# A two-layer transformer with 16 experts on one core: another order of work where the first expert stage opens, two weight tiles more, another last pair

## The chip, the core and the metric

The kernel runs on one core of a Trainium2 chip. The metric is device time in microseconds (us): 1926.18, the median of three runs (1924.14 to 1932.64). Five engines matter: TensorE (PE), VectorE (DVE), ScalarE (ACT), GpSimd (POOL) and SyncE (SP), which issues most of the transfers. About 0.5% of the time, 9.6 us, is what a measurement of this kernel can tell from no change.

## The reference

Two layers work on 512 latent tokens (`x`) and 256 context tokens (`ctx`) of width 1024. The second layer has no context output.

```
for l in range(2):
    need_ctx = l < 1
    mod_l = silu(c) @ w_mod[l] + b_mod[l]          # six vectors of 1024, and so for the context
    h_l = modulate(rms_norm(x, norm1_g[l]), sh1, sc1)
    y_l, y_c = token_mixer(h_l, h_c, w_in[l], ..., w_out[l], need_ctx)
    x = x + g1 * y_l
    h_l = modulate(rms_norm(x, norm2_g[l]), sh2, sc2)
    x = x + g2 * expert_choice_ffn(h_l, w_router[l], w_gate[l], w_up[l], w_down[l])
    if need_ctx: the same for ctx, with its own g1, sh2, sc2, g2
return rms_norm(x, final_g)

def expert_choice_ffn(h, ...):                     # 16 experts, each picks its best tokens
    aff = softmax(h @ w_router);  gate, idx = top_k(aff.T, cap)    # cap 64 latent, 32 context
    a, u = xs @ w_gate, xs @ w_up                  # xs = h[idx], matrices of 1024 x 1024
    y = (silu(a) * u) @ w_down * gate              # scattered back by idx, sums of all experts
```

All is float32. One layer's expert matrices are 16 x 3 x 4 MB.

## The kernel before

The program goes through six stages: the opening (loads, modulation vectors, norms), layer 0's mixer, layer 0's experts, and the same for layer 1 without an opening. Experts are taken two at a time, eight pairs `p` a layer.

**Weights.** Class `Ring` (L1426) streams the expert matrices. One load is half the rows (`kh`) of one expert's matrix, 128 partitions x 16 KB, 2 MB; two loads (both experts of the pair) make a half matrix. The loads' order is gate of pair 0, then up `p`, gate `p+1`, down `p` (`ring_loads`, L1415). They rotate through tiles: in layer 0 three in pool `ra` and three in `rb`, six. I count them from 0: loads 0 to 3 are gate of pair 0, 4 to 7 up of pair 0, 8 to 11 gate of pair 1, 12 to 15 down of pair 0. Load 6 takes load 0's tile. SP issues them in this order, and each waits until TensorE has read its tile for the last time.

**Expert stage of layer 0** (`experts`, L1181, with `two`). TensorE's order is written out. For pair 0 the latent gate product is made ahead (`gate0`, L1134, `ps_g`); in the stage itself come the first half of up (`ps_u`), the transposes of the context's gathered rows (`xsc`), the context's gate product (`ps_gc`), the second half of up, and the context's up product (`ps_uc`). Then pairs 1 to 7 go through gate, down and up, each half matrix with latent (`lat_mm`, L1117) and context (`cx_mm`, L1127) columns. Results of pairs 0 to 5 are scattered with addition into memory (`scatter`, L1287), those of 6 and 7 are added from PSUM (`add`, L1330) to `xe`, which is loaded after pair 5.

**Before that stage** stands the end of layer 0's mixer: the output projection (`acc`), `out_add` (L884), and for each stream the router: `Norm2` (L893) with squares on ACT, transposes `ps_t`, logits `ps_lg`, `softmax`, then `top` (L964, repeated max, replace and index of eight on DVE), and `slots_l` / `slots_c` (L998, L1030), which make the row indices by small matmuls `ps_r`. The latent selection ends first, its first gather is `xsl` and its transposes and modulation give `xT0`. The context's selection is woven between the matmuls of `gate0` by a scheduler; its scratch, its tile `xc` and the weight staging of the mixer lie in memory that the expert stage's pool `ep` takes over.

**Opening** (L1506 to L1530). SP loads six tiles `xt` of x and ctx (L284), small rows (`c`, `c_ctx`, `norm1_g`, `norm2_g`, `conv_w`, `final_g`) into tile `rows`, and then the modulation weights `wm` (L220) into four rotating buffers. `norm2_g` comes by four transfers that put every fourth number into a row (L1515). One transpose turns `rows` into `cols`, silu of which is `cT`, the operand of all modulation products `ps_mod` (`mod_half`, L210). ACT's six squares of `xt` and DVE's reciprocal roots (`rsqrt`, L171, 14 small instructions) normalise the tiles.

**Last pair of layer 1** (L1388 to L1407, `last_pair` L1145). The loop's last steps are `down(6)`, `up(7)`, `add(6)`, the transposes of the product (`turned(7)`), and `down(7)`. Between the halves of `down(7)` TensorE multiplies six of the eight 128x512 pieces of `x` by the identity into PSUM (`residual`):

```
PE.matmul(xa[t, h], ident, R.x[:, t, 512 * h:512 * h + 512], start=True, stop=False)
```

On top of them come the last pair's sums `yH` and `yL` (the high and the low part of the result). Two pieces are summed on DVE. Then follow squares on ACT, a reciprocal root for token tiles 0 and 1 and another for 2 and 3, the last product with `final_g` (five pieces on DVE, three on ACT and POOL), and eight stores.

Of the kernel before, what the change touches and what calls it, by code (L numbers as in the profile page):

```python
# [60 lines left out]
NACC = 6  # L61
FINE = (9, 10, 11, 12)
# [26 lines left out]
def kernel(ctx_stack: ExitStack, tc: tile.TileContext, x, c, ctx, c_ctx, w_mod, b_mod, norm1_g,  # L89
# [802 lines left out]
    class Norm2:  # L892
# [8 lines left out]

        def half(self, nh):
            s, p, pp, x, R = self.s, self.p, self.pp, self.x, self.R
            for t in range(NT[s]):
                xs = x[:, t, 512 * nh:512 * nh + 512]
                junk = p.tile([128, 512], BF, name="junk", tag="s2", bufs=S2O)
                ACT.activation(junk, xs, AF.Square, accum_out=self.sq[:, nh, t:t + 1])
                ps = pp.tile([128, 4, 128], F32, name="ps_t", tag="t", bufs=2)
                for j in range(4):
                    PE.transpose(ps[:, j], xs[:, j::4], ident)  # L910
                h = p.tile([128, 4, 128], F32, name="hsc", tag="s2", bufs=S2O)
                if t % 2:
                    DVE.tensor_copy(h, ps)
                else:
                    ACT.activation(h, ps, AF.Copy)
                yield
                for j in range(4):

                    js = slice(32 * j, 32 * j + 32)
                    PE.matmul(self.lg[js, 128 * t:128 * t + 128], R.wrA[s][:, 4 * nh + j, :], h[:, j],  # L920
                              start=(nh == 0 and t == 0), stop=(nh == 1 and t == NT[s] - 1), tile_position=(0, 32 * j))
                yield
# [211 lines left out]
    def gate0(gp, pp, ring, xl):  # L1134

        G = [pp.tile([128, 512], F32, name="ps_g", tag="acc", bufs=4) for _ in range(2)]
        W = [ring.get2() for _ in range(2)]
        for k in range(KC):
            lat_mm(G, xl, k, k % 4, W[k // 4], 64)
        sil = gp.tile([128, D], F32, name="sil0")  # L1140
        for h in range(2):
            ACT.activation(sil[:, 512 * h:512 * h + 512], G[h], AF.Silu)
        return sil, W

    def last_pair(ep, eq, pp, R, OH, yH, yL, xa, fg):  # L1145
# [14 lines left out]
        for t0 in range(0, NL, 2):  # L1160
            ts = slice(t0, t0 + 2)
            for t in range(t0, t0 + 2):
                for h in range(2):
                    junk = eq.tile([128, 512], BF, name="junk", tag="sil", bufs=1)
                    ACT.activation(junk, src[t, h], AF.Square, accum_out=m[:, 0, h, t:t + 1])
            DVE.tensor_tensor(m[:, 1, 0, ts], m[:, 0, 0, ts], m[:, 0, 1, ts], OP.add)
            rsqrt(m[:, 2, 0, ts], m[:, 1, 0, ts], m[:, 1, 1, ts], 1.0 / D)
# [12 lines left out]
    def experts(l, ep, ring, pp, R, xe, streams, late):  # L1180
# [15 lines left out]
        xT, sil, silc, aT, aTc, Y, G, GC, first, xs = {}, {}, {}, {}, {}, {}, {}, {}, [], {}  # L1196
# [43 lines left out]
        def up(p):  # L1240
            U = [ptile("ps_u", "b") for _ in range(2)]
            UC = ptile("ps_uc", "bc") if two else None
            for _ in matrix(U, UC, xT["l", p], two and lhs_c(xT["c", p], p)):
                pass
# [42 lines left out]
        def scatter(p, Dn, DC):  # L1287

            y = ep.tile([128, D], F32, name="y", tag=("yH", "yL")[p % 2], bufs=1)
# [11 lines left out]
            if p == NACC - 1:  # L1301
                for s in streams:
                    POOL.dma_start(xe[s], xres_d[s].rearrange("(t p) d -> p t d", p=128))

        def down(p, fill=None):
# [540 lines left out]
```

## Time and profile before

| | us |
|---|---|
| median of three runs | 1926.18 |
| the profiled execution, its own time | 1925.89 |
| its span, first to last instruction | 1924.1 |
| PE busy | 1783.6 (93%) |
| DVE busy | 664.1 (35%) |
| ACT busy | 481.9 (25%) |
| POOL busy | 321.1 (17%) |

| stage | from | to |
|---|---|---|
| opening, up to the first products of the mixer | 0 | 40 |
| layer 0's mixer and selection | 40 | 537 |
| layer 0's experts | 537 | 1060 |
| layer 1's mixer and selection | 1060 | 1440 |
| layer 1's experts and the last pair | 1440 | 1924 |

Layer 0's experts, in the 40 us from 800 to 840: PE busy 39.77, DMA 397 GB/s. Layer 1's experts, from 1600 to 1640: PE busy 38.66, DMA 430 GB/s. A matmul's end is modelled, so a busy PE may still be one that waits a little between instructions. The time that an engine waits for nothing visible is called issue.

### The profile page before, as it was taken

Reading aid. Unit: us, or ns where it says so; the run is one execution under the profiler, and the core shown is the slowest. Engines: PE = TensorE matmul, PEld = TensorE weight load, DVE = VectorE, ACT = ScalarE, POOL = GpSimd, SP = SyncE. Lnnn points to the kernel's source line nnn. Section 1 sums busy time; section 2 is a strip of 40 time slices with the busy share of each in tenths; the row PEclk is TensorE's granted clock in tenths of the full one; section 3 lists DMA queues with packets and bytes.
Section 4 is the critical chain, followed back from the end, with each engine's and each line's share of the span. In section 5 each row is a group of like instructions: output and inputs, shape, how many; then the busy total and the mean of one; then the engine's idle time right before and its main releaser. Section 6 shows DMA issues by size and latency. Waiting matters only on the chain. (4 is left out here: it accounts for less than half of the span.)

```text
span 1924.1 us, 30120 instructions
## 1 busy us (share of the span) xinstructions
PE 1783.6 (93%) x12613; PEld 1023.5 (53%) x12613; DVE 664.1 (35%) x1681; ACT 481.9 (25%) x965; POOL 321.1 (17%) x335
## 2 busy tenths in 40 slices
PE   4899999999889999999999889999969999999986
PEld 2787887767423333333323588887744444544432
DVE  5645435673611101011003655446341122221214
ACT  3344434353401001000000445454331000000001
POOL 3233123333200111011000233223410000000000
PEclk9999999999889999999999899999979999999998
DMA  7554264257659999999997411110747999999993
GB/s 236 167 198 166 91 205 155 88 187 291 272 214 422 410 410 415 417 399 401 402 412 318 155 45 42 59 34 34 294 176 277 427 429 430 430 430 429 429 429 145
DMA packets 90351, 527.63 MB, mean 274 GB/s; under 512 B 11300, under 2 KB 33880, under 8 KB 66408
## 3 DMA queue, kind: packets, MB, share of 16 engines
q1 hardware_dynamic: 84808, 511.24, 66.4%
q0 software_dynamic: 5408, 14.47, 2.6%
q8 instruction: 99, 1.62, 0.3%
q14 instruction: 36, 0.29, 0.0%
HBM read 510.41 MB, written 15.27 MB: 273 GB/s over the span
## 5 line engine op out<-in xcount | busy, mean ns | idle before, releaser
L1124 PE MATMUL ps_u<-ring,xTl 128*32 128x512 f32 (+1 forms) x1536 | 243.3, 601 | 14.2 <-DMA ring<-in_w_up_dram 13.5
L1124 PE MATMUL ps_g<-ring,xTl 128*32 128x512 f32 (+1 forms) x1472 | 239.0, 594 | 4.0 <-DMA ring<-in_w_gate_dram 2.8
L1124 PE MATMUL ps_d<-ring,aT 128*32 128x512 f32 (+1 forms) x1536 | 237.3, 593 | 2.5 <-DMA ring<-in_w_down_dram 2.1
L1124 PEld LDWEIGHTS ps_u<-ring,xTl 128*32 128x32 f32 (+1 forms) x1536 | 71.9, 120 | 169.3 <-issue 146.6
L1257 ACT ACTIVATE aT<-ps_t 128x512 f32<-128x512 f32 x16 | 9.6, 598 | 607.1 <-PE ps_t L1253 607.1
L353 PE MATMUL acc<-wH,hHl 128*128 128x256 f32 x512 | 152.4, 298 | 3.2 <-ACT wH L274 1.8
L1124 PEld LDWEIGHTS ps_g<-ring,xTl 128*32 128x32 f32 (+1 forms) x1472 | 74.3, 121 | 149.5 <-issue 130.5
L354 PE MATMUL acc<-wH,hLl 128*128 128x256 f32 x512 | 145.1, 283 | 3.2 <-DVE hLl L343 3.2
L1124 PEld LDWEIGHTS ps_d<-ring,aT 128*32 128x32 f32 (+1 forms) x1536 | 70.8, 119 | 145.0 <-issue 136.9
L355 PE MATMUL acc<-wL,hHl 128*128 128x256 f32 x512 | 145.6, 284 | 1.4 <-DVE wL L275 1.3
L353 PEld LDWEIGHTS acc<-wH,hHl 128*128 128x128 f32 x512 | 98.1, 192 | 30.8 <-issue 23.7
L1236 DVE TENSOR_TENSOR sil<-ps_u,sil 128x512 f32<-128x512 f32 x32 | 22.1, 692 | 244.6 <-PE ps_u L1124 233.4
L275 POOL TENSOR_TENSOR wL<-wraw,wH 128x512 fp32r<-128x512 f32 x44 | 57.5, 1308 | 275.1 <-ACT wH L274 253.6
L355 PEld LDWEIGHTS acc<-wL,hHl 128*128 128x128 f32 x512 | 98.1, 192 | 4.4 <-DVE wL L275 2.7
L354 PEld LDWEIGHTS acc<-wH,hLl 128*128 128x128 f32 x512 | 98.1, 192 | 4.1 <-DVE hLl L343 4.1
L1255 DVE COPY aT<-ps_t 128x512 f32<-128x512 f32 x16 | 11.1, 691 | 252.3 <-PE ps_t L1253 252.3
L1175 POOL TENSOR_TENSOR x<-z,xTl 128x512 f32<-128x512 f32 x3 | 4.2, 1412 | 501.8 <-ACT z L1174 501.8
L677 DVE TENSOR_REDUCE mc<-ps_s 128x1 f32<-128x513 f32 (+2 forms) x80 | 55.2, 690 | 84.3 <-PE ps_s L674 53.0
L679 ACT ACTIVATE P<-ps_s,mc 128x513 f32<-128x513 f32 (+2 forms) x80 | 55.1, 689 | 95.4 <-DVE mc L677 95.3
L274 ACT ACTIVATE wH<-wraw 128x512 fp32r<-128x512 f32 x88 | 55.0, 629 | 91.7 <-PE acc L354 43.4
L1114 PE MATMUL ps_x<-OT,xn 128*128 128x128 f32 x512 | 67.1, 297 | 8.1 <-DVE OT L1106 8.1
L1131 PE MATMUL ps_uc<-ring,xTc 128*32 128x512 f32 x512 | 72.9, 592 | 0.0
(492 smaller groups left out, 3201.3 us busy)
## 6 DMA issues: line engine op xcount, KB each, us to landing
ring<-in_w_up_dram SPq DMA_DIRECT2D x64, 2048.0 KB
ring<-in_w_gate_dram SPq DMA_DIRECT2D x61, 2048.0 KB
ring<-in_w_down_dram SPq DMA_DIRECT2D x61, 2048.0 KB
wm<-in_w_mod_dram SPq DMA_DIRECT2D x96, 512.0 KB
wraw<-in_w_in_dram SPq DMA_DIRECT2D x44, 512.0 KB
wraw_o<-in_w_out_dram SPq DMA_DIRECT2D x24, 512.0 KB
ring<-in_w_gate_dram SPq DMA_DIRECT2D x12, 512.0 KB
ring<-in_w_down_dram SPq DMA_DIRECT2D x12, 512.0 KB
```

The lines of the kernel that those rows point to most:

```text
L274: ACT.activation(H, src, AF.Copy)
L275: sub_eng().tensor_sub(L, src, f32(H))
L353: PE.matmul(ps, aH, bH, start=start, stop=False)
L354: PE.matmul(ps, aL, bH, start=False, stop=False)
L355: PE.matmul(ps, aH, bL, start=False, stop=stop)
L677: DVE.tensor_reduce(mc[:, 0:1], sc, AX.X, OP.max, negate=True)
L679: ACT.activation(P[:, :nk + 1], sc, AF.Exp, bias=mc[:, 0:1], accum_out=mc[:, 1:2])
L1114: PE.matmul(ps[:, j], R.xn[:, t, c0:c0 + 128], OT[:, t], start=(t == 0), stop=(t == 3))
L1124: PE.matmul(G[h][c:c + n], lhs[:, k, c:c + n], W[e][:, j, 512 * h:512 * h + 512], start=(k == 0), stop=(k == KC - 1), tile_position=(0, c))
L1131: PE.matmul(gcx[32 * b:32 * b + 32], lhs_c(k, e), W[e][:, j, 512 * h:512 * h + 512], start=(k == 0), stop=(k == KC - 1), tile_position=(0, ...
L1236: DVE.tensor_mul(sil[p][:, hs], U[h], sil[p][:, hs])
L1255: DVE.tensor_copy(aT[p][:, 4 * h:4 * h + 4], ps)
```

## The change

Four things change.

- **Opening.** `norm2_g` comes by one transfer of four rows of 512 numbers into a tile of its own, `rows2`, and four more transposes pick every fourth number. POOL clears `rows` first.
- **Selection.** TensorE's order in the opening of layer 0's expert stage is written out (`open_pairs`): the context's router transposes and logits, its softmax, the transposes of `xsl`, then `gate0` in three parts: two of its eight steps, the transposes of the affinities, four steps, the context's slots, two steps.
- **Ring.** Loads 6 and 7 get tiles of their own, in `ep`, of two halves each (four transfers of 1 MB). Rotation through the six tiles goes on with load 8. Later the same memory holds `y` and `xe`.
- **Last pair.** `add(6)` moves between the halves of `up(7)`. The identity products are gone: all eight sums are added to `x` on DVE, the last square is DVE's, and one reciprocal root serves all four token tiles.

```diff
+G0 = (2, 4)
...
-                    for i in range(4):
-                        SP.dma_start(rows[32 + 4 * i:36 + 4 * i], norm2_g[i // 2, 512 * (i % 2):512 * (i % 2) + 512]
-                                     .rearrange("(p j) -> j p", j=4))
+                    rows2 = p.tile([4, 512], F32, name="rows2", tag="s2", bufs=S2)
+                    SP.dma_start(rows2, norm2_g.rearrange("l (k n) -> (l k) n", n=512))
...
                     PE.transpose(ps[:, :68], rows, ident[:68, :68])
+                    for j in range(4):
+                        PE.transpose(ps[:, 128 + 4 * j:132 + 4 * j], rows2[:, j::4], ident[:4, :4])
                     DVE.tensor_copy(cols, ps[:, :68])
+                    DVE.tensor_copy(cols[:, 32:48].rearrange("p (b j) -> p b j", j=4),
+                                    ps[:, 128:144].rearrange("p (j b) -> p b j", j=4))
...
+                        def open_pairs():
+                            hs, todo = {}, [(h, t) for h in range(2) for t in range(2)]
+                            for i, ht in enumerate(todo):
+                                hs[ht] = nc2.turn(*ht)
+                                if i:
+                                    nc2.logits(*todo[i - 1], hs[todo[i - 1]])
+                            nc2.logits(*ht, hs[ht])
                             nc2.softmax()
-                            yield from keep("c", nc2, xc)
-                            slots_c(rp, pp, R, (yield from top(p, pp, R, "c", 32)), ra[0])
-                        aft = select_c()
+                            R.xT0 = columns(l, "l", R.xs0, ra[0], 1,
+                                            lambda nm: pp.tile([128, 512], F32, name=nm, tag="t", bufs=2))
+                            drain(keep("c", nc2, xc))
+                            g0 = gate0(ra[0], pp, ring, R.xT0, R)
+                            for _ in range(G0[0]):
+                                next(g0)
+                            tp = top(p, pp, R, "c", 32)
+                            next(tp)
+                            for _ in range(G0[1]):
+                                next(g0)
+                            try:
+                                while True:
+                                    next(tp)
+                            except StopIteration as e:
+                                slots_c(rp, pp, R, e.value, ra[0])
+                            drain(g0)
...
+                if self.n in self.extra:
+                    parts = self.extra.pop(self.n)
+                    for i, t in enumerate(parts):
+                        SP.dma_start(t, src[:, 2 * i:2 * i + 2])
+                    self.q[self.n] = Halves(parts)
+                    self.n += 1
+                    continue
...
+                if two:
+                    for i in range(2):
+                        ring.extra[6 + i] = [ep.tile([128, 2, D], F32, name="ring", tag=f"o{i}{j}", bufs=1)
+                                             for j in range(2)]
...
-                ps = xa[t, h] if t < 3 else pp.tile([128, 512], F32, name="ps_s", tag="a", bufs=2)
-                PE.matmul(ps, o_, yH[:, hs], start=(t == 3), stop=False)
+                ps = bank("ps_s")
+                PE.matmul(ps, o_, yH[:, hs], start=True, stop=False)
                 PE.matmul(ps, o_, yL[:, hs], start=False, stop=True)
-                src[t, h] = ps
-                if t == 3:
-                    src[t, h] = R.x[:, t, hs]
-                    DVE.tensor_add(src[t, h], src[t, h], ps)
+                src[t, h] = R.x[:, t, hs]
+                DVE.tensor_add(src[t, h], src[t, h], ps)
...
-                up(p + 1)
-            add(6)
+                up(p + 1, (lambda: add(6)) if p == 6 and not two else None)
+            if two:
+                add(6)
...
-            down(7, residual)
-            last_pair(ep, E[0], pp, R, OH, *Y[7], xa, fg)
+            down(7)
+            last_pair(ep, E[0], bank, R, OH, *Y[7], fg)
```

Where layer 0's expert stage opens, TensorE had this order before (a row is one line's matmuls in turn; `xsl` are the gathered latent rows, `xc` the context, `ps_lg` logits, `aff_c` affinities):

```order
L1088 MATMUL ps_t<-ident,xsl 128x128 x8
L1124 MATMUL ps_g<-ring,xTl 64x512
L910 MATMUL ps_t<-ident,xc 128x128 x8
L1124 MATMUL ps_g<-ring,xTl 64x512 x2
L920 MATMUL ps_lg<-hsc,wrAc 32x128 x8
L910 MATMUL ps_t<-ident,xc 128x128 x8
L1124 MATMUL ps_g<-ring,xTl 64x512 x2
L920 MATMUL ps_lg<-hsc,wrAc 32x128 x8
L1124 MATMUL ps_g<-ring,xTl 64x512 x2
L933 MATMUL ps_r<-qsum,lgs 128x16 x2
L1124 MATMUL ps_g<-ring,xTl 64x512 x6
L981 MATMUL ps_r<-ident,aff_c 16x128 x2
```

and has this one now:

```order
L911 MATMUL ps_t<-ident,xc 128x128 x8
L1026 MATMUL ps_r<-ident,tok_l 64x8 x2
L1026 MATMUL ps_r<-ident,val 64x8 x2
L1030 MATMUL ps_r<-ident,tok_l 64x8
L923 MATMUL ps_lg<-hsc,wrAc 32x128 x4
L911 MATMUL ps_t<-ident,xc 128x128 x4
L923 MATMUL ps_lg<-hsc,wrAc 32x128 x4
L911 MATMUL ps_t<-ident,xc 128x128 x4
L923 MATMUL ps_lg<-hsc,wrAc 32x128 x8
L942 MATMUL ps_r<-qsum,lgs 128x16 x2
L1097 MATMUL ps_t<-ident,xsl 128x128 x8
L1133 MATMUL ps_g<-ring,xTl 64x512 x8
```

The context's router now stands whole ahead of the gate products, and its first transposes even ahead of the latent slots (`tok_l`); before, 13 of the 32 gate matmuls stood ahead of the affinities, now 8.

At the end of the program, TensorE's order before, from the last sum of `add(6)` on (`sil` is the product of gate and up):

```order
L1338 MATMUL ps_s<-yH,OH 128x512
L1339 MATMUL ps_s<-yL,OH 128x512
L1253 MATMUL ps_t<-ident,sil 128x128 x8
L1124 MATMUL ps_d<-ring,aT 64x512 x16
L1405 MATMUL ps_x<-x,ident 128x512 x6
L1124 MATMUL ps_d<-ring,aT 64x512 x16
L1154 MATMUL ps_x<-yH,OH 128x512
L1155 MATMUL ps_x<-yL,OH 128x512
```

and now:

```order
L1355 MATMUL ps_s<-yH,OH 128x512
L1356 MATMUL ps_s<-yL,OH 128x512
L1133 MATMUL ps_u<-ring,xTl 64x512 x16
L1263 MATMUL ps_t<-ident,sil 128x128 x8
L1133 MATMUL ps_d<-ring,aT 64x512 x32
L1165 MATMUL ps_s<-yH,OH 128x512
L1166 MATMUL ps_s<-yL,OH 128x512
```

The second half of `up(7)` now follows `add(6)`, and nothing stands between the halves of `down(7)`. Elsewhere each engine's order is as before, but for ACT and DVE in the opening: ACT's last three squares of `xt` now follow the silu that makes `cT`, and DVE's copies into `cols` stand inside the first reciprocal root.

## Rows read from the trace of the kernel before

**Rows 1.** Timeline of SP, 0 to 48: start, us, engine, line, operation
```profile
5.59 9.91 SPq L1515 DMA_DIRECT2D rows<-in_norm_g_dram  x4
...
17.75 13.43 SPq L220 DMA_DIRECT2D wm<-in_w_mod_dram  x10
```
**Rows 2.** Stretch, us; busy PE, PEld, DVE, ACT, POOL; PEclk, DMA share, GB/s
```profile
12.00:14.00 2.00, 0.00 (x0) 0.00 (x0) 0.00 (x0) 1.57 (x3) 0.00 (x0) 1.00 0.26 2
```
**Rows 3.** Timeline of PE, 500 to 600; in brackets idle time before, and its releaser
```profile
512.83 1.98 PE L1088 MATMUL ps_t<-ident,xsl 128*128 128x128 f32 x8 [5.19 <-DMA xsl<-xn_l,idx_l]
...
519.38 1.23 PE L910 MATMUL ps_t<-ident,xc 128*128 128x128 f32 x8
...
523.14 0.62 PE L933 MATMUL ps_r<-qsum,lgs 128*128 128x16 f32 x4
...
537.24 7.07 PE L1124 MATMUL ps_u<-ring,xTl 128*32 128x512 f32 x64 [0.69 <-ACT sil L1142]
...
562.02 9.51 PE L1124 MATMUL ps_u<-ring,xTl 128*32 128x512 f32 x59 [3.12 <-DMA ring<-in_w_up_dram]
...
580.06 1.92 PE L1124 MATMUL ps_g<-ring,xTl 128*32 128x512 f32 x16
```
**Rows 4.** Stretches of 2 us, columns as in rows 2
```profile
564.00:566.00 2.00, 2.00 (x12) 0.39 (x8) 0.00 (x0) 0.00 (x0) 0.00 (x0) 0.50 0.98 418
...
574.00:576.00 2.00, 2.00 (x24) 0.54 (x20) 0.00 (x0) 0.00 (x0) 0.00 (x0) 1.00 0.00 0
```
**Rows 5.** Timeline of SP, 480 to 640
```profile
549.28 0.81 SPq L1463 DMA_DIRECT2D ring<-in_w_up_dram  x2
```
**Rows 6.** Timeline of PE, 1835 to 1925
```profile
1869.16 7.08 PE L1124 MATMUL ps_u<-ring,xTl 128*64 128x512 f32 x30 [2.61 <-DMA ring<-in_w_up_dram]
...
1880.06 1.35 PE L1253 MATMUL ps_t<-ident,sil 128*128 128x128 f32 x8
...
1888.57 5.42 PE L1405 MATMUL ps_x<-x,ident 128*128 128x512 f32 x12
1893.92 7.09 PE L1124 MATMUL ps_d<-ring,aT 128*64 128x512 f32 x32
```
**Rows 7.** Timeline of DVE, 1835 to 1925
```profile
1876.93 4.87 DVE L1340 TENSOR_TENSOR x<-x,ps_s 128x512 f32<-128x512 f32 x8
...
1901.73 1.45 DVE L1319 TENSOR_TENSOR yL<-ps_d,yH 128x512 fp32r<-128x512 f32 x2
...
1907.06 0.16 DVE L1166 TENSOR_TENSOR fm<-fm 128x2 f32<-128x2 f32 x1 [0.17 <-ACT junk L1165]
...
1909.62 0.75 DVE L1177 SCALAR_TENSOR_TENSOR x<-ps_x,fm,xTl 128x512 f32<-128x512 f32 x1
...
1915.81 2.41 DVE L1177 SCALAR_TENSOR_TENSOR x<-x,fm,xTl 128x512 f32<-128x512 f32 x2
```
**Rows 8.** Timeline of ACT, 0 to 48
```profile
10.79 1.06 ACT L296 ACTIVATE junk<-xt 128x1024 bf16<-128x1024 f32 x1 [0.22 <-DMA xt<-in_ctx_dram]
...
12.41 1.06 ACT L296 ACTIVATE junk<-xt 128x1024 bf16<-128x1024 f32 x1 [0.47 <-DMA xt<-in_ctx_dram]
```
**Rows 9.** Timeline of DVE, 0 to 48
```profile
20.19 0.23 DVE L1521 COPY cols<-ps_t 128x68 f32<-128x68 f32 x1 [8.34 <-PE ps_t L1520]
...
26.48 1.42 DVE L302 TENSOR_SCALAR xt<-xt,rstd 128x1024 f32<-128x1024 f32 x2
```
**Rows 10.** Timeline of POOL, 496 to 590
```profile
506.10 1.26 POOL L890 TENSOR_TENSOR xc<-xc,ty 128x512 f32<-128x512 f32 x1 [1.67 <-DVE ty L889]
...
509.49 1.27 POOL L890 TENSOR_TENSOR xc<-xc,ty 128x512 f32<-128x512 f32 x1
```
**Rows 11.** Stretch of 1 us near the end, columns as in rows 2
```profile
1889.00:1890.00 1.00, 1.00 (x4) 0.41 (x3) 0.00 (x0) 0.00 (x0) 0.00 (x0) 1.00 0.17 66
```
**Rows 12.** Timeline of ACT, 1835 to 1925
```profile
1908.50 0.63 ACT L1165 ACTIVATE junk<-x 128x512 bf16<-128x512 f32 x1
```
**Rows 13.** Timeline of POOL, 1835 to 1925
```profile
1910.63 2.49 POOL L1175 TENSOR_TENSOR x<-z,xTl 128x512 f32<-128x512 f32 x2 [498.90 <-ACT z L1174]
```

More of the change, by code (lines that the diff above doesn't have):

```diff
@@ L900, in __init__, with turn, logits @@
             self.lg = pp.tile([128, 512], F32, name="ps_lg", tag="lg", bufs=1)
-        def half(self, nh):
[L903 to L915, printed above, removed]
+        def turn(self, nh, t):
+            p = self.p
+            xs = self.x[:, t, 512 * nh:512 * nh + 512]
+            junk = p.tile([128, 512], BF, name="junk", tag="s2", bufs=S2O)
+            ACT.activation(junk, xs, AF.Square, accum_out=self.sq[:, nh, t:t + 1])
+            ps = self.pp.tile([128, 4, 128], F32, name="ps_t", tag="t", bufs=2)
+            for j in range(4):
+                PE.transpose(ps[:, j], xs[:, j::4], ident)
+            h = p.tile([128, 4, 128], F32, name="hsc", tag="s2", bufs=S2O)
+            if t % 2:
+                DVE.tensor_copy(h, ps)
+            else:
+                ACT.activation(h, ps, AF.Copy)
+            return h
+        def logits(self, nh, t, h):
+            for j in range(4):
+                js = slice(32 * j, 32 * j + 32)
+                PE.matmul(self.lg[js, 128 * t:128 * t + 128], self.R.wrA[self.s][:, 4 * nh + j, :], h[:, j],
+                          start=(nh == 0 and t == 0), stop=(nh == 1 and t == NT[self.s] - 1), tile_position=(0, 32 * j))
+        def half(self, nh):
+            for t in range(NT[self.s]):
+                h = self.turn(nh, t)
                 yield
[L917 to L921, printed above, removed]
+                self.logits(nh, t, h)
                 yield
@@ L1238, in times, with up @@
                 DVE.tensor_mul(silc[p], UC, silc[p])
[L1240 removed]
+        def up(p, fill=None):
             U = [ptile("ps_u", "b") for _ in range(2)]
             UC = ptile("ps_uc", "bc") if two else None
[L1243 removed]
+            for _ in matrix(U, UC, xT["l", p], two and lhs_c(xT["c", p], p), fill=fill):
                 pass
@@ L1301, in scatter, with down @@
             if p == NACC - 1:
-                for s in streams:
-                    POOL.dma_start(xe[s], xres_d[s].rearrange("(t p) d -> p t d", p=128))
-        def down(p, fill=None):
+                y2 = ep.tile([128, 2, D], F32R, name="yHL", tag="o00", bufs=1)
+                last.extend(y2[:, i] for i in range(2))
+                xr = [ep.tile([128, 2, D], F32, name="xe", tag=f"o{g}", bufs=1) for g in ("01", "10", "11")]
+                xe["l"], xe["c"] = Halves(xr[:2]), xr[2]
+                for i, s in enumerate("llc"):
+                    POOL.dma_start(xr[i], xres_d[s][256 * (i == 1):256 * (i == 1) + 256, :].rearrange("(t p) d -> p t d", p=128))
+        def down(p):
             Dn = [ptile("ps_d", "a") for _ in range(2)]
             DC = ptile("ps_dc", "ac") if two else None
-            for _ in matrix(Dn, DC, aT[p], lambda k, e: aTc[p][:, k % 4, 2 * e + k // 4, :], fill=fill):
+            for _ in matrix(Dn, DC, aT[p], lambda k, e: aTc[p][:, k % 4, 2 * e + k // 4, :]):
                 pass
@@ L1369, in experts @@
                     cx_mm(UC, lc, k, k % 4, W1[k // 4])
+                y2 = ep.tile([128, 2, D], F32, name="y", tag="o00", bufs=1)
+                ys.extend(y2[:, i] for i in range(2))
                 silu(0)
@@ L1510 @@
                     rows = p.tile([68, 128], F32, name="rows", tag="s2", bufs=S2)
+                    POOL.memset(rows, 0.0)
                     SP.dma_start(rows[0:8], c.rearrange("b (r p) -> (b r) p", p=128))
```

63 lines of the change are left out of this document (34 added, 29 removed).

## The prediction

> **What bounds the kernel now.** I read the page's shares first: PE is busy for 93% of the span. So only stretches in which PE waits, or works at half speed, can give time, and there are three of them that the change touches.
>
> The first is the start. SP's timeline shows the four `norm2_g` transfers at 5.59, holding SP for 9.91 us, and the first `wm` issued at 17.75 [rows 1]. In the stretch from 12 to 14 the DMA moves 2 GB/s [rows 2]: nothing of weight is under way, and PE has nothing to multiply.
>
> The second is layer 0's expert opening. PE's timeline shows the order of things and the waits: `xsl` transposes at 512.83, first `ps_u` at 537.24, then the second half of up held by DMA (the last of its waits is 3.12) until 562.02, and pair 1's gate at 580.06 [rows 3]. The windows show the rest: at 564 to 566 PE works at a granted clock of 0.50, and at 574 to 576 no DMA runs although PE is full [rows 4]. So loads 6 and 7 came too late, not too slowly. SP issued them at 549.28 [rows 5]: they sit in the tiles of loads 0 and 1, which the context's gate product reads until then. After this stage opens, PE is full (39.77 of 40 us in the table above), so what PE gains here stays gained. Layer 1's experts run at the DMA's pace instead, but their loads follow the mixer's end and move with it as a block.
>
> The third is the end. PE's timeline has a wait of 2.61 for up's second half at 1869.16, then `add(6)` behind it, then 5.42 us of identity products between the halves of `down(7)` [rows 6]. DVE's timeline has the tail behind the last product at 1901.01 [rows 7].
>
> The profiled execution took 1925.89, 0.29 below the median of the runs; I make the sum against it.
>
> **Start: 5.5 less.** The four transfers go, and one of four long rows comes, which I cost like its neighbours: below 1 us of SP's time. In the built order SP then waits, before each further transfer, for an earlier one to complete; the first `wm` stands behind the first context tile. That tile had landed at 10.79, the other at 12.41 [rows 8]. So `wm` starts up to 17.75 − 10.79 = 7.0 earlier. That is the upper end. What may not keep up is the normalised x, which PE transposes among the products. Before, `rows` were copied at 20.19, and the last tile was scaled from 26.48 in two of 1.42, done by 27.9 [rows 9]: 7.7 us in all, beside `wm` transfers that hid it. After the change ACT makes three of the six squares behind `cT`, so at best they come at 12.41 + 1.5 (landing of the rows, the transposes) + 3 × 1.25 = 17.7, and DVE then needs 7.7 less one early pair's 1.3, until 24.1: 3.8 earlier than 27.9. This is the lower end while DVE is late. PE has products of its own to put between, so I take the middle, 5.5. The four extra transposes, the second copy and POOL's clearing lie in the wait for the first weights; bare, they would cost under 1 us.
>
> **Opening of the experts: 14.2 less.** Here PE's order is fixed, so I lay it out in the trace's time. The context's last sums are made on POOL; the first tile's end at 507.36, the last piece at 509.49 + 1.27 = 510.76 [rows 10]. The transposes of the first now stand ahead of the latent slots. Half of 1.23 behind 507.36 is 508.0, some 0.85 later for the slots by my estimate, and so for POOL's gather and last sum behind them: 511.6. From there to the softmax's products stand four transposes, a copy, eight logits matmuls. In the trace the stretch from 519.38 to 523.14 + 0.62 holds all that and eight gate products of 0.22 [rows 3] [rows 6]: 4.4 with them, 2.6 without. I take 4.0: the `xsl` transposes begin at 515.6, 2.8 later than before, and end at 517.5 (1.98 for eight, against 1.35 for eight at the end of the program, so at the low clock).
>
> Then gate 0: 64 products at 7.09 for 32, 14.2. I add 1.3 for a start at the low clock, 1.2 for two groups of small products between its parts (0.62 for such a group), 0.7 for silu as before: `ps_u` at 534.9, against 537.24. From there to pair 1's gate stand four products of 64 at 7.07 and two sets of transposes at 1.35: 31.0 without a wait, so 565.9 where the trace has 580.06. **That is 14.2.**
>
> Is the load there? Loads 6 and 7 lie in memory that the context's scratch holds until the context's slots are made. Those stand behind six of the eight gate steps on PE: 517.5 + 1.3 + 0.6 + 6 × 1.77 = 530.0, so I put the issue at 530.5. They need 10 us for 4 MB at the 418 GB/s of [rows 4], so they land by 541 to 543, with the two gathers among them. The second half of up wants them behind 534.9 + 7.07 + 1.35 + 7.07, at 550.4. Seven us are spare. Load 8 and the later ones then find their tiles free as before, and the DMA, idle at 574 to 576, has its work earlier. The context's gather, delayed by that traffic, is wanted only at 542. SP's queue holds the two loads ahead of gate 1's, which could not start before 549 anyway.
>
> Bounds: without lateness and low clock, 512.83 + 1.98 + 14.2 + 1.2 + 0.7 + 31.0 = 561.9, which is 18.2 less. At half clock through all of gate 0, 12.9 more than I reckon: 1.3 less.
>
> **End: 7.9 less.** `add(6)` took 3.8 (1876.24 to 1880.06) and moves into the wait of 2.61: the second half of up starts at 1866.55 + 3.8 instead of 1869.16 and ends at 1877.4. Its product takes 0.7, the transposes and copies 1.5: `down(7)` starts at 1879.6 instead of 1881.56. DVE's sums of pair 6 (4.87 for eight) now run beside PE. With the identity products' 5.4 gone, the last product ends at 1893.6 instead of 1901.0, 7.4 earlier. The last weights don't hold it: from 1889 to 1890 the last 66 GB/s come in [rows 11], and the last quarter of the second half is read only after 1891.
>
> The tail: before, from the last product to DVE's last one 17.2, and 5.9 of stores behind. After (E is the last product): both sums' parts by E + 2.2 as now, eight sums at 0.61 until E + 7.1, seven squares on ACT, 0.63 each [rows 12] and 0.75 with their read-out, until E + 8.1, a reciprocal root of 2.56 until E + 10.7, then five products on DVE. All of them now read `x` and `final_g` from SBUF. From PSUM one took 0.75; the two from SBUF took 2.41, 1.2 each, beside POOL's sum. POOL's two of 1910.63 took 2.49 [rows 13]. Five at 1.2 end at E + 16.7: 0.5 less than before. All at 0.75 would give 2.8 less; five of these and three of POOL's one after another, 3.8 + 3.7, end at E + 18.2: 1.0 more. I take 0.5 less, the rows' own price.
>
> That last case is a rule of the Trainium skill, "SBUF — State Buffer", section "SBUF: two separate sides": a VectorE operation with two SBUF inputs and a GpSimd operation hold their shared port pair in turn, each blocking the other for its whole length. By it the end would give 6.4 in place of 7.9, and the sum 1899.8. The 2.41 agrees with some blocking, not with a full turn each.
>
> The loads of `xe` in three transfers, and `y` in one tile, lie beside PE's full stretch and cost nothing as long as PE does not wait there.
>
> **Sum:** 5.5 + 14.2 + 7.9 = 27.6. 1925.9 − 27.6 = **1898.3**.
>
> **Rivals.**
> - *The start is absorbed.* DVE's normalising, late behind `cT`, is then what PE waits for, and the gain is nil: 1903.8. For it: DVE's 7.7 us; against it: PE has the products first.
> - *Gate 0 stays slow.* The selection in front leaves PE mostly idle, and gate 0 runs at the low clock: 1.3 in place of 14.2, so 1911.2. For it: `xsl` transposes at 1.98. Against it: PE is dense from 517.5 on.
> - *Only the end holds.* The loads come no earlier, since the memory stays held by something that I overlooked, or layer 1 takes back what layer 0 gives: 1918.0, within 0.5%.
> - *Slower: the low clock through the whole opening.* If the small steps keep PE at half speed for gate 0 and the four products behind it, 14.2 + 4 × 7.07 − 1.3 = 41.2 more turn 27.6 into −13.6: 1939.5. It decides from 27.6 us of lost speed on. Against it: at 564 to 566 the clock was 0.50 after a wait, and at 574 to 576 it was 1.00 again [rows 4].
>
> The Trainium skill, "TensorE: Matmul & The Clock Gate", Part 1, says that the slow clock is the default and that activity lifts it. By that rule a thinner stretch ahead of gate 0 costs time, which the last and the second rival price from rows; the 0.50 at 564 to 566, behind a wait, agrees.
>
> **How the numbers follow.** Forecast 0.65, start absorbed 0.14, gate 0 slow 0.12, only the end 0.06, slower 0.03. The forecast's own bounds: all upper ends give 7.0 + 18.2 + 10.2 = 35.4, so 1890.5. The range goes from there to 1911, which takes in the first rival and half of the second. About 0.5%, 9.6 us, is what a measurement can tell from no change: faster 0.91, same 0.06, slower 0.03.
>
> **What would show it.** `wm` from 11 on and the first `ps_mod` by 16; loads 6 and 7 issued near 525 (all that follows the start is 5.5 earlier), no DMA wait in the second half of up, pair 1's gate near 560; both halves of `down(7)` end to end; the tail about 22.6 from the last product to the end. It is wrong if PE's first transposes of x wait for DVE, if a granted clock of 0.50 lasts through gate 0, if the loads are issued only where the gate's tiles come free, or if DVE's last products and POOL's sums alternate in full.

## The result, and the profile after

The changed kernel took 1898.55 us in the median of four runs (1895.8 to 1900.76), the kernel before 1927.58 beside it. The ratio is 0.9847, with a 95% interval of 0.982 to 0.9874. Measured once more with the last experiments it took 1899.8 against 1924.56, a ratio of 0.9874 (0.9858 to 0.9889). The forecast was 1898.3.

| | before | after |
|---|---|---|
| the profiled execution, its own time | 1925.89 | 1895.8 |
| its span | 1924.1 | 1894.0 |
| PE busy | 1783.6 | 1772.5 |
| POOL busy | 321.1 | 323.1 |

**The start.** SP's timeline of the changed kernel from 0 to 48: the one `norm2_g` transfer takes 0.25 where four held SP for 9.91, and the first `wm` goes out at 10.34 instead of 17.75 [rows 1].

```profile
5.48 0.25 SPq L1546 DMA_DIRECT2D rows<-in_norm_g_dram  x1
7.72 0.30 SPq L1547 DMA_DIRECT2D rows<-in_conv_w_dram  x1
9.06 0.27 SPq L1548 DMA_DIRECT2D rows<-in_final_g_dram  x1
10.34 17.08 SPq L221 DMA_DIRECT2D wm<-in_w_mod_dram  x10
```

From 12 to 14 the DMA moves 260 GB/s instead of 2 [rows 2]. TensorE's timeline of the same stretch:

```profile
15.57 7.30 PE L225 MATMUL ps_mod<-wm,cT 128*32 128x512 f32 x20 [0.67 <-ACT cT L1557]
...
23.41 0.33 PE L309 MATMUL ps_t<-ident,xt 128*128 128x128 f32 x1 [0.17 <-DVE xt L303]
24.67 0.33 PE L309 MATMUL ps_t<-ident,xt 128*128 128x128 f32 x1 [0.93 <-DVE xt L303]
25.62 0.41 PE L309 MATMUL ps_t<-ident,xt 128*128 128x128 f32 x2 [0.62 <-DVE xt L303]
...
34.89 0.39 PE L354 MATMUL acc<-wH,hHl 128*128 128x256 f32 x1 [1.20 <-ACT wH L275]
```

Here are three waits on DVE's normalising, 1.7 together. The prediction named such waits as a sign that it is wrong; the gain came all the same. The last row is the first product of the mixer; it stood at 40.24 before. The 7.30 of the modulation products ahead of the waits are mostly waits as well: TensorE's weight loads (PEld) show 1.77, 1.11, 1.15 and 1.47 for `wm`, 5.5 together. The first of these rows and the last:

```profile
17.53 0.19 PEld L225 LDWEIGHTS ps_mod<-wm,cT 128*32 128x32 f32 x4 [1.77 <-DMA wm<-in_w_mod_dram]
...
21.82 0.14 PEld L225 LDWEIGHTS ps_mod<-wm,cT 128*32 128x32 f32 x4 [1.47 <-DMA wm<-in_w_mod_dram]
```

**The opening of the experts.** TensorE's timeline from 485 to 600, to be read beside [rows 3]:

```profile
509.75 1.95 PE L1097 MATMUL ps_t<-ident,xsl 128*128 128x128 f32 x8
511.63 4.32 PE L1133 MATMUL ps_g<-ring,xTl 128*64 128x512 f32 x16
...
516.20 7.09 PE L1133 MATMUL ps_g<-ring,xTl 128*64 128x512 f32 x32
...
528.16 7.07 PE L1133 MATMUL ps_u<-ring,xTl 128*32 128x512 f32 x64 [0.70 <-ACT sil L1152]
...
543.40 7.05 PE L1133 MATMUL ps_u<-ring,xTl 128*32 128x512 f32 x64
...
558.55 1.92 PE L1133 MATMUL ps_g<-ring,xTl 128*32 128x512 f32 x16
```

The second half of up starts without a wait, and pair 1's gate at 558.55 instead of 580.06. SP's timeline has loads 6 and 7, in four parts, 16 us ahead of the gate's loads; the windows show full speed and a busy DMA where [rows 4] had a clock of 0.50 and a DMA at rest:

```profile
523.93 2.17 SPq L1476 DMA_DIRECT2D ring<-in_w_up_dram  x4
540.19 4.24 SPq L1493 DMA_DIRECT2D ring<-in_w_gate_dram  x4
```

```profile
543.00:545.00 2.00, 2.00 (x24) 0.62 (x20) 0.00 (x0) 0.60 (x1) 0.00 (x0) 1.00 0.98 418
552.00:554.00 2.00, 2.00 (x24) 0.64 (x20) 0.00 (x0) 0.00 (x0) 0.00 (x0) 1.00 1.03 442
```

**The end.** TensorE's timeline (as [rows 6]), and below it its weight loads, which show what the first product of `down(7)` waits for:

```profile
1835.54 7.08 PE L1133 MATMUL ps_u<-ring,xTl 128*64 128x512 f32 x30 [2.42 <-DMA ring<-in_w_up_dram]
...
1846.52 7.09 PE L1133 MATMUL ps_u<-ring,xTl 128*64 128x512 f32 x32
1853.54 1.60 PE L1263 MATMUL ps_t<-ident,sil 128*128 128x128 f32 x8
1855.07 1.07 PE L1133 MATMUL ps_d<-ring,aT 128*64 128x512 f32 x2
1856.97 13.95 PE L1133 MATMUL ps_d<-ring,aT 128*64 128x512 f32 x62 [0.82 <-DMA ring<-in_w_down_dram]
```

```profile
1856.96 0.20 PEld L1133 LDWEIGHTS ps_d<-ring,aT 128*64 128x64 f32 x4 [1.70 <-DMA ring<-in_w_down_dram]
```

`add(6)` stands between 1842.6 and 1846.5 as planned, and both halves of `down(7)` run end to end. New is the wait of 1.70 for down's weights, which the prediction did not have. DVE's and POOL's timelines of the tail:

```profile
1872.98 4.86 DVE L1168 TENSOR_TENSOR x<-x,ps_s 128x512 f32<-128x512 f32 x8
...
1881.56 6.42 DVE L1187 SCALAR_TENSOR_TENSOR x<-x,fm,xTl 128x512 f32<-128x512 f32 x5
```

```profile
1882.36 5.07 POOL L1185 TENSOR_TENSOR x<-z,xTl 128x512 f32<-128x512 f32 x3 [494.69 <-DVE x L1187]
```

DVE's five products are of two kinds, as the list of their lengths in ns (least, median, most) shows: 0.75 us before POOL starts, 1.75 beside it. Each engine's queue closes the program with instructions called DRAIN (L1900). POOL's longest lasts 8267 ns. It begins at 1884.9 and ends at 1893.2, 5.7 behind POOL's last product; SP is at its first DRAIN, behind the stores, at 1891.0:

```profile
L1187 DVE SCALAR_TENSOR_TENSOR x<-x,fm,xTl x5: 744/1746/1750, 1881.6 to 1886.2; 128x512 f32<-128x512 f32 x5
L1900 POOLq DRAIN  x3: 51/97/8267, 1884.9 to 1893.7; - x3
L1900 SPq DRAIN  x3: 7/7/7, 1891.0 to 1893.4; - x3
```

**Where the time went.** The same program does not put its stages at the same time in each execution, so I compare distances inside one execution. The marks are: the first product of the mixer; the last product of the context's output projection (505.78 before, 500.01 after); the first `ps_u` of pair 0; pair 1's gate; the first half of `up(7)`; the end of the last `ps_d`; the span's end.

| stretch | before | after | gain | forecast |
|---|---|---|---|---|
| to the mixer's first product | 40.24 | 34.89 | 5.35 | 5.5 |
| to the output projection's last | 465.54 | 465.12 | 0.4 | 0 |
| to the first up | 31.46 | 28.15 | 3.3 | 2.3 |
| to pair 1's gate | 42.82 | 30.39 | 12.4 | 11.9 |
| to `up(7)` | 1279.4 | 1277.0 | 2.4 | 0 |
| to the last `ps_d`'s end | 41.55 | 35.38 | 6.2 | 7.4 |
| to the span's end | 23.1 | 23.1 | 0.0 | 0.5 |

(The forecast's 14.2 of the opening is split here by its own numbers: 537.24 − 534.9 = 2.3, and the rest, 14.2 − 2.3 = 11.9.) This is one pair of executions; three of its rows look different over all runs, as the experiments show: the start, the end, and the stretch to `up(7)`.

### The profile page after: what moved, and what is told of

Its sections match the earlier page's. It is cut to its first block, busy times and chain, and to the rows that moved or that the text cites. A ratio compares the mean times of both kernels' runs of the same rounds, so it can differ in the third digit from the quotient of the medians.

```text
span 1894.0 us, 30111 instructions
## 1 busy us (share of the span) xinstructions
PE 1772.5 (94%) x12605; PEld 1017.2 (54%) x12605; DVE 664.9 (35%) x1676; ACT 480.9 (25%) x963; POOL 323.1 (17%) x337
## 5 line engine op out<-in xcount | busy, mean ns | idle before, releaser
L1133 PE MATMUL ps_u<-ring,xTl 128*32 128x512 f32 (+1 forms) x1536 | 238.8, 592 | 4.1 <-DMA ring<-in_w_up_dram 3.4
```

The source lines that it names most:

```text
L1133: PE.matmul(G[h][c:c + n], lhs[:, k, c:c + n], W[e][:, j, 512 * h:512 * h + 512], start=(k == 0), stop=(k == KC - 1), tile_position=(0, c))
```

## The experiments

Eleven variants and the changed kernel once more. Times are medians; the kernel before is the one of the same call.

| run | us | before | ratio (95%) |
|---|---|---|---|
| 1 order alone | 1911.17 | 1925.29 | 0.9925 (0.9909 to 0.9942) |
| 2 tiles alone | 1901.51 | 1925.29 | 0.9874 (0.9858 to 0.9891) |
| 3 old start | 1901.56 | 1925.29 | 0.988 (0.9863 to 0.9896) |
| 4 old end | 1906.9 | 1925.29 | 0.9903 (0.9883 to 0.9923) |
| 5 normalising first | 1900.78 | 1924.4 | 0.9875 (0.9859 to 0.9892) |
| 6 `add(6)` back | 1900.7, one run | 1924.4 | |
| 7 tail on DVE | 1896.78, one run | 1924.4 | |
| 8 `down(7)` in quarters | 1899.86 | 1924.4 | 0.9869 (0.9853 to 0.9886) |
| 9 squares first | 1900.94, one run | 1924.56 | |
| 10 = 7 and 8 | 1896.28 | 1924.56 | 0.9851 (0.9836 to 0.9867) |
| 11 = 10, `up(7)` in quarters | 1896.74 | 1924.56 | 0.9846 (0.9827 to 0.9864) |
| 12 changed kernel again | 1899.8 | 1924.56 | 0.9874 (0.9858 to 0.9889) |

### 1 and 2: order of work or tiles?

Run 1 takes the two tiles away; run 2 weaves the context's selection into gate 0 as before, with the tiles.

```diff
-                    for i in range(2):
-                        ring.extra[6 + i] = [ep.tile([128, 2, D], F32, name="ring", tag=f"o{i}{j}", bufs=1)
-                                             for j in range(2)]
+                    pass
```

> The changed kernel without the two extra weight tiles: TensorE's new order stays, loads 6 and 7 go back to the tiles of loads 0 and 1. Theory (the tiles carry most of the opening's 15.7 us): the loads are issued only when the context's gate product has read the first tiles, near 540, the second half of up ends some 12 us later than in the changed kernel, pair 1's gate starts near 570 instead of 558.6, and the profiled time is near 1908. Rival (the order carries it): pair 1's gate within 4 us of 558.6, time below 1900.

```diff
-                        def open_pairs():
...
+                        def select_c():
+                            for h in range(2):
+                                yield from nc2.half(h)
+                            nc2.softmax()
+                            yield from keep("c", nc2, xc)
+                            slots_c(rp, pp, R, (yield from top(p, pp, R, "c", 32)), ra[0])
+                        aft = select_c()
```

> The changed kernel with the old weaving of the context's selection into gate 0, but with the two extra tiles. Theory: up starts 3.3 us later than in the changed kernel (near 531.5), loads 6 and 7 are issued near 527.5 and arrive in time, pair 1's gate starts near 562, and the profiled time is near 1899. Rival (without the order the tiles' memory comes free too late): a wait on DMA in the second half of up, pair 1's gate after 566, time above 1903.

TensorE's timeline of run 1, then of run 2:

```profile
530.86 7.07 PE L1133 MATMUL ps_u<-ring,xTl 128*32 128x512 f32 x64 [0.70 <-ACT sil L1152]
...
550.73 1.92 PE L1133 MATMUL ps_u<-ring,xTl 128*32 128x512 f32 x2 [4.45 <-DMA ring<-in_w_up_dram]
555.59 9.01 PE L1133 MATMUL ps_u<-ring,xTl 128*32 128x512 f32 x59 [2.94 <-DMA ring<-in_w_up_dram]
...
573.12 1.92 PE L1133 MATMUL ps_g<-ring,xTl 128*32 128x512 f32 x16
```

```profile
532.16 7.07 PE L1133 MATMUL ps_u<-ring,xTl 128*32 128x512 f32 x64 [0.69 <-ACT sil L1152]
...
547.41 7.05 PE L1133 MATMUL ps_u<-ring,xTl 128*32 128x512 f32 x64
...
562.55 1.92 PE L1133 MATMUL ps_g<-ring,xTl 128*32 128x512 f32 x16
```

The two parts separate cleanly at the first up. Ahead of it, from the output projection's last product (502.63 and 499.85 in these runs), run 1 takes 28.2, as the changed kernel, and run 2 takes 32.3, about as before (31.5). Behind it, to pair 1's gate, run 1 takes 42.3, as before (42.8), and run 2 takes 30.4, as the changed kernel. So the order is worth 3 to 4, the tiles 12, and neither needs the other. Both theories held in their main number; run 2's up came 4.2 later than in the changed kernel, counted from that product, where I expected 3.3, and its loads did not come too late.

### 3 and 4: the old start and the old end

> The changed kernel with the old four element-wise norm2_g transfers. Theory: the first product of the mixer moves from 34.9 back to 40.2 and everything behind it by 5 to 6 us; the profiled time is near 1901.5. Rival (the mixer absorbs a late start): the output projection's last product within 2 us of the changed kernel's 500.0, time below 1898.

> The changed kernel with the old end: add(6) behind up(7), identity products between the halves of down(7), old last sums. Theory: all of the end's gain sits in TensorE's part, so the last product of down(7) ends 6.2 us later (near 1877.1), the tail behind it is 23.1 as in both, and the profiled time is near 1902. Rival (the tail on DVE costs what PE gains): the tail is shorter than 22 us and the time is below 1900.

Run 3 puts the four element-wise transfers back (the lines of the change's first part, undone); its first mixer product starts at 38.99, and from the output projection's last product on the distances are those of the changed kernel (58.5 to pair 1's gate). The shift was 4.1 where I expected 5.3. Its median is 1901.56, as expected.

Run 4 puts the old last pair back. From `up(7)` to the last `ps_d`'s end it takes 41.6, as before. The changed kernel's profile has 35.4 there, and six others with the changed end (runs 1, 2, 3, 5, 9 and 12) have 34.6 to 34.8. So the end gains 6.9 as a rule; the 6.2 of the table is the one low profile. It takes 23.2 from there to the end: what the end gains, it gains on TensorE, and the new tail on DVE costs as much as the old. The median, 1906.9, is 7.1 to 8.4 above the changed kernel's two. But the profiled execution is above what I expected (its span is 12.3 longer than the changed kernel's, not 6.2). The difference was there before the end: the first mixer product started at 38.09, though the program is the same up to there. The windows of run 4 show it:

```profile
24.00:26.00 2.00, 0.66 (x2) 0.28 (x2) 1.96 (x5) 0.21 (x1) 0.00 (x0) 0.98 0.94 322
26.00:28.00 2.00, 1.63 (x6) 0.48 (x6) 0.89 (x2) 0.38 (x1) 0.00 (x0) 0.50 0.98 373
28.00:30.00 2.00, 2.00 (x10) 1.14 (x6) 0.72 (x2) 0.25 (x1) 0.00 (x0) 0.50 0.14 46
30.00:32.00 2.00, 2.00 (x10) 0.20 (x8) 0.99 (x2) 0.14 (x1) 0.00 (x0) 0.50 0.81 255
```

TensorE was busy for 0.66 of 2 us while it waited for x; then the granted clock fell to 0.50, 1.2 GHz, until after 32. In the changed kernel's own profile the same waits ended with the clock still at 1.00.

Over all profiles with the new start on SP as in the change the first mixer product lies between 34.4 and 38.1 (ten profiles, median 35.7); with the old start it lay at 40.24 and 38.99. So the start's gain is some 4 at that mark, and 5.35 is the pair that happened to be profiled. Part of the spread is a wait that I overlooked. In runs 6, 7, 8, 11 and 12 (35.5 to 36.4) ACT waited 0.2 to 1.7 for the mixer's first weights, `wraw`, which SP issues behind the ten `wm`; in the four at 34.4 to 35.0 it did not. ACT's timeline of run 7:

```profile
35.74 1.15 ACT L275 ACTIVATE wH<-wraw 128x512 fp32r<-128x512 f32 x2 [1.72 <-DMA wraw<-in_w_in_dram]
```

By the end of the mixer less is left. The output projection's last product lies at 499.9 to 505.2 in the ten profiles, median 503.0, against 505.8 and 505.4 with the old start: 2.6. Between 24 and 67 the granted clock stood at 0.50 for 3.4 us with the old start (before, run 3), and so in the changed kernel's profile and run 2; in the other eight it did for 6.8 or 10.2.

The stretch from pair 1's gate to `up(7)` varies too: 1276.8 to 1280.9 in the runs with the changed loads there, and 1279.4 before. The 2.4 in the table above are no effect that I can show.

### 5 and 9: is it DVE that holds the start?

> The changed kernel with the six squares of xt put ahead of silu on ACT (the normalising is written ahead of the small rows). Theory (DVE's late normalising now holds TensorE's start, and the waits let its clock fall): the waits of the x transposes on xt (0.36 and less to 0.93, some 1.7 together) are gone, no stretch between 24 and 34 shows a granted clock of 0.50, and the first product of the mixer starts near 33.2, against 34.9 in the changed kernel and 38.1 in the run with the old end. Rival (the wm transfers hold it): waits on DMA wm take their place and the first product of the mixer is within 0.5 of 34.9.

Run 5 wrote the whole normalising ahead of the small rows. It did more than was meant: two `wm` went ahead of the rows on SP, and the identity came later on DVE. TensorE's first transposes waited for DVE until 16.33 and the first `ps_mod` came at 19.67. The waits on x were gone, but so was the start's gain (first mixer product 39.14): nothing follows for the question. Run 9 moves the squares alone:

```diff
+                    ms = squares(xn, (p, "s2", S2))
                     ps = pp.tile([128, 512], F32, name="ps_t", tag="t", bufs=4)
                     PE.transpose(ps[:, :68], rows, ident[:68, :68])
...
-                    norm_x(xn, None, (p, "s2", S2))
+                    norm_x(xn, None, (p, "s2", S2), ms)
```

> The changed kernel with ACT's six squares of xt ahead of silu; the small rows and the first four wm stay where they are on SP, the two rope tables come before the later wm. Theory (DVE's late normalising holds TensorE's start): the waits of the x transposes on xt (1.7 in the changed kernel) vanish, no stretch between 24 and 34 has a granted clock under 0.9, and the first product of the mixer starts at 34.0 or earlier, against 34.4 to 36.4 in the runs with the new start (38.1 once). Rival (the wm transfers hold it): waits on DMA wm take their place and the first product of the mixer starts at 34.5 or later.

```profile
18.72 4.68 PE L225 MATMUL ps_mod<-wm,cT 128*32 128x512 f32 x12 [1.18 <-DMA wm<-in_w_mod_dram]
23.67 1.54 PE L225 MATMUL ps_mod<-wm,cT 128*32 128x512 f32 x4 [0.28 <-DMA wm<-in_w_mod_dram]
25.14 0.87 PE L320 MATMUL ps_t<-ident,xt 128*128 128x128 f32 x6
```

The six transposes run without a wait on DVE, and waits on the weights stand ahead of them: 1.18 + 0.28. The first mixer product came at 34.98, as in the changed kernel. The rival holds in this variant: with DVE out of the way, the `wm` transfers set the pace. But its edit also puts the two rope tables among them on SP, which the changed kernel loads only at 41.56. The changed kernel's own trace has the waits of 5.5 for `wm` ahead of those for DVE. What freeing DVE alone would gain, no run shows.

### 6 and 8: what the end waits for

Run 6 puts `add(6)` back behind `up(7)`; run 8 loads the first half of `down(7)` in quarters, both experts in turn:

```diff
-                up(p + 1, (lambda: add(6)) if p == 6 and not two else None)
-            if two:
-                add(6)
+                up(p + 1)
+            add(6)
```

> The changed kernel with add(6) back behind up(7), still without identity products. By the recorded sum the last product of down(7) ends 2.0 later, counted from the start of the first half of up(7): 37.4 instead of 35.4. Rival (down(7)'s weights have become the wait, 0.96 to 1.70 on TensorE's weight loads in these runs, and add(6) fills that wait): only 0.8 to 1.6 later, 36.2, and no wait on DMA at the start of down(7).

```diff
-                fine = l and (self.n in FINE or self.n >= 94)
+                fine = l and (self.n in FINE or self.n >= 92)
```

> The changed kernel with the first half of down(7) also loaded in quarters, both experts in turn, as its second half is. Theory (TensorE waits there for the second expert's whole 2 MB): the wait of 0.96 to 1.70 on TensorE's weight loads in front of down(7) goes, and from the start of the first half of up(7) to the last product's end it takes 33.7 to 34.2 instead of 34.6 to 35.4. Rival (the DMA's pace is the bound): the wait moves to a later quarter, and the distance stays within 0.3 of 34.6 to 35.4.

TensorE's weight loads in run 6, then in run 8:

```profile
1839.76 0.20 PEld L1133 LDWEIGHTS ps_u<-ring,xTl 128*64 128x64 f32 x4 [3.59 <-DMA ring<-in_w_up_dram]
1849.47 0.20 PEld L1133 LDWEIGHTS ps_u<-ring,xTl 128*64 128x64 f32 x4 [1.81 <-DMA ring<-in_w_up_dram]
```

```profile
1862.13 0.14 PEld L1133 LDWEIGHTS ps_d<-ring,aT 128*64 128x64 f32 x2 [0.28 <-DMA ring<-in_w_down_dram]
```

In run 6 the last product ended 36.1 after the start of `up(7)`, 0.7 later than in the changed kernel's profile and 1.5 later than in run 12 (34.6), not the 2.0 of my sum. That is still 5.5 less than the 41.6 of the old end: the products with the identity that the change drops, 5.4 in the sum, gave what they had cost. The wait moved in front of `up(7)`'s second half, and `down(7)` waits for no DMA. In run 8 the wait in front of `down(7)` shrank from 1.70 (0.93 to 1.07 in runs 1, 2, 3, 5, 9 and 12) to 0.28, and the distance is 33.5. So the wait was for the second expert's whole 2 MB, and smaller pieces remove most of it. The median, 1899.86, does not show the 1.1 or more that this saves in the trace.

### 7: the tail on DVE alone

```diff
-FIN = ((0, 1), (1, 1), (2, 1))
+FIN = ()
```

> The changed kernel with all eight final products on DVE, none on ACT and POOL. Theory (the 1.28 of a product comes from sharing the port with POOL): each takes 0.62 to 0.75, eight take 5.0 to 6.0 instead of 6.42 for five, and the last product of DVE ends 0.4 to 1.4 earlier after the last product of down(7), 16.0 instead of 17.1. Rival (two SBUF operands make a DVE product slow by themselves): 8 x 1.28 = 10.2, the tail 3.8 longer.

DVE's timeline of run 7:

```profile
1886.32 5.39 DVE L1187 SCALAR_TENSOR_TENSOR x<-x,fm,xTl 128x512 f32<-128x512 f32 x8
```

Eight products take 5.39, 0.67 each; the five of the changed kernel took 6.42, two of them before POOL started and three beside it, 1.7 apart. DVE's last product ends 16.0 after the last `ps_d`, as expected. The span ends 19.2 after it, 3.9 earlier than with POOL, where I expected 1: from DVE's last product to the end it is 3.2, against 6.0. Run 10 repeats it (19.2), and run 12 has the other (23.0).

The closing rows tell where the 3.9 lie. 1.1 are DVE's products, which end sooner. The other 2.8 are POOL's DRAIN, which in run 7 ran hundreds of us earlier: POOL's last operation there is a clearing of 0.3 ahead of layer 1's experts, and the DRAIN of 6.0 begins with it at 1390.8. The end follows SP's first DRAIN by 0.9:

```profile
L1900 POOLq DRAIN  x3: 51/97/6039, 1390.8 to 1894.6; - x3
L1900 SPq DRAIN  x3: 7/7/7, 1894.0 to 1894.3; - x3
```

In every profile with POOL in the tail its long DRAIN ends 5.6 or 5.7 behind POOL's last product, and the span 0.8 behind the DRAIN, with SP done 2 us sooner; the kernel before is one of them. Run 7 takes ACT's part of the tail away together with POOL's, but ACT's first DRAIN is over at 1884.9 in the changed kernel: it isn't what the end waits for. Why POOL's DRAIN takes so long, no row tells.

By the Trainium skill, "SBUF — State Buffer", section "SBUF: two separate sides", a VectorE operation with two SBUF inputs and a GpSimd operation that reads SBUF hold their shared port pair in turn. The trace agrees nearly: one product and one POOL sum in full turns would take 0.67 + 1.25 = 1.92 (1.25 is half of [rows 13]'s 2.49), and beside each other a pair takes 1.7.

### 10 to 12: a version that beats both

> The changed kernel with all final products on DVE and down(7)'s first half in quarters. If both savings add up: from the last product of down(7) to the span's end 19.2 instead of 23.1, from the start of up(7) to that product 33.5 instead of 34.6 to 35.4, so 5 to 6 less than the changed kernel, near 1893. Rival (the 3.9 of the tail was one run's luck): the tail is 22 or more and the time within 2 of the changed kernel's.

> As the run before, with up(7) in quarters too. Theory (TensorE's wait of 2.4 in front of up(7) is for whole 2 MB loads): that wait becomes shorter than 1, but the DMA's end bounds the last product, so the time is at most 1 less than with down(7) alone, unless the wait also lowered the clock (8.78 instead of 7.08 for the first half in two runs), which is then gone. Rival (four small transfers in place of one cost the DMA pace): the last product of down(7) later by 1 or more.

> The changed kernel as it is, beside the two runs before on the same chip. Expected near 1898.5, with 23.1 from the last product of down(7) to the span's end and the first product of the mixer between 34.4 and 38.1.

Run 10 took 1896.28 and run 12, the changed kernel, 1899.8: 3.5 less, where I expected 5 to 6. That is under what one measurement of this kernel tells apart, but the traces show the tail's share twice, 19.2 against 23.0 to 23.1. Of the other half, the wait ahead of `down(7)` shrank again, to 0.29, but the distance did not: the first half of `up(7)`, behind its wait of 2.4 on DMA, took 8.78 instead of 7.08 in the profile of run 10, so the distance to the last product is 35.2; without these 1.7 it is run 8's 33.5. The granted clock there, from 1840 to 1842, was 0.50:

```profile
1840.00:1842.00 2.00, 2.00 (x6) 0.49 (x4) 0.00 (x0) 0.00 (x0) 0.00 (x0) 0.50 1.04 438
```

Run 11 had no wait ahead of `up(7)`, but TensorE now waits for each quarter of `down(7)`'s second half:

```profile
1870.25 0.20 PEld L1133 LDWEIGHTS ps_d<-ring,aT 128*64 128x64 f32 x4 [1.09 <-DMA ring<-in_w_down_dram]
...
1872.79 0.20 PEld L1133 LDWEIGHTS ps_d<-ring,aT 128*64 128x64 f32 x4 [1.07 <-DMA ring<-in_w_down_dram]
...
1875.32 0.20 PEld L1133 LDWEIGHTS ps_d<-ring,aT 128*64 128x64 f32 x4 [1.06 <-DMA ring<-in_w_down_dram]
```

The last product is set by the DMA's end, as I expected. The small transfers did not slow the queue: from the issue of pair 7's gate to the last byte of weights it took 88.1, and 87.5 to 89.0 in runs 8, 10 and 12. Its median, 1896.74, is the same as run 10's.

## Why the prediction was right, point by point

- **The start, 5.5.** The size held in the profiled pair (5.35); over all profiles it is some 4 at the mixer's first product and 2.6 at its end. That 5.5 was the middle between a shift of 3.8 and one of 7.0; the mechanism did not give it, so the close hit is partly luck. The sign that the prediction gave for being wrong, transposes of x that wait for DVE, came true at 1.7 and did not undo the gain. What holds TensorE there is not DVE alone: waits of 5.5 for `wm` stand ahead, and in half of the profiles one for `wraw` behind. The low clock that followed those waits in run 4 was priced for the experts' opening only, not here: a rival for the start was missing.
- **The opening, 14.2.** It is 15.7, and its two halves stand apart as the sum had them. The selection in front put the `xsl` transposes 2.7 later from the output projection's last product (I reckoned 2.8); the first quarter of gate 0 ran at the low clock for 0.8 more (4.32 for 16 products, 3.55 at full speed; I had 1.3); loads 6 and 7 were issued at 523.9, where the shifted forecast said 525. The rest is that small products between gate 0's parts took less than 1.2, and that four products of 64 follow each other 6.9 apart, not 7.07. The rival of a gate 0 at half clock fell: 7.09 for the next 32 products is full speed.
- **The end, 7.9 with the tail's 0.5.** The 7.4 of TensorE were 6.2 in the profiled pair and 6.9 in six other profiles. The step that failed is "the last weights don't hold it". I looked at the last quarter of the second half and not at the first half's second load, which had landed before TensorE asked for it only as long as `add(6)` stood in front. The wait of 1.70 in the profile, of about 1 in six others, is that load. The products with the identity gave what the sum has for them (run 6). So the move of `add(6)` gave 0.7 to 1.5, not 2.0, and part of the cost that it hid came back as a wait one step later.
- **The tail, 0.5 less.** It came out even, 23.1 and 23.1. The step that failed is the 5.9 of stores behind DVE's last product. SP is done with the stores at 1891.0; the end waits for POOL's DRAIN until 1893.2, so what counts is POOL's last product, 16.7 behind the last `ps_d` before and 16.5 after. The 1.2 for a product, too, is the mean of [rows 7]'s two, of which one ran free (0.74) and one beside POOL (1.75). The alternation of DVE and POOL that the prediction names as a sign of being wrong nearly came: a pair of both takes 1.7, where full turns take 1.92. DVE's five products took 6.42, 0.4 more than five of 1.2.
- **The sum.** 27.6 forecast, 30.1 in the profiled pair, 29.0 and 24.8 between the medians of the two measurements. It came out by an opening that was 1.5 too small and an end with its tail 1.7 too large. With the distances that most profiles show, 2.6 at the start, 15.7 in the opening, 6.9 at the end and nothing in the tail, it is 25.2. That the median of the first measurement lies 0.3 from the forecast is therefore partly luck: the forecast takes its gain from one execution of 1925.89, while the median beside it was 1927.58.

## What to carry to other kernels

Where a stage is held by a load that waits for a buffer, ask which memory comes free earlier for other reasons: here scratch of the selection, dead before the stage that needs the load, carried 12 of the opening's 16 us. When work is moved into a wait on DMA, the next load in the same queue becomes the wait; look one load further before the whole wait is counted as gain. And compare distances between marks inside one execution: one run of a program can start its stages 4 us later than another of the same program.

## What the runs showed that I had not expected

- A final product on POOL costs more than its time beside DVE. Without POOL in the tail, the span ended 3.2 after DVE's last product instead of 6.0. In the changed kernel the stores' last bytes move between 1890 and 1891; until 1893.2 the program waits for POOL's DRAIN. By these numbers, as an estimate, POOL's last product would have to end 3.3 before DVE's to be free; here it ends 0.6 before it.
- The clock after a short wait is not the same in each run of the same instructions. After a wait of 2.4 on DMA, the first half of `up(7)` took 7.08 in seven of the new kernels' profiles (and once more behind a wait of 0.8, in run 9) and 8.78 or 8.79 in four (runs 4, 6, 7 and 10; in 4 and 6 the next wait on DMA, 0.9 where it was 2.6, took most of it up). In the stretch from 24 to 34, with the waits for x, one of ten profiles worked at 0.50 for 6 us; runs 6, 8 and 11 show such a stretch between 35 and 42.
